# A streaming-encoder block on one core: the planned order's rule for the port that VectorE and GpSimd share, gating and pooling matrices in fp32, and two pieces of GpSimd's work given to VectorE

## The chip, the cores and the metric

The kernel runs on one NeuronCore of a Trainium2 chip. The core has a matrix engine (TensorE, "PE" in the profile, with its weight loads shown apart as "PEld"), VectorE ("DVE"), ScalarE ("ACT"), GpSimd ("POOL") and SyncE ("SP"), whose queue issues every DMA of this kernel. Each engine takes its instructions strictly in the order in which the program gives them; semaphores make an engine wait for others. The metric is the device time in microseconds of one execution; lower is better. The kernel before takes 1183.75 us (median of 3 runs, 1181.96 to 1185.1).

## The reference, cut to what matters

One layer of an encoder over 1024 positions of 1024 channels, all in fp32. Three sub-layers follow one another, each normalised before and after and added to the stream. The change touches the first one, and of the second the weights of its values.

```python
h = rms_norm(x, pre_mix_g)                 # 1024 x 1024
z = h @ w_in + b_in                        # columns: A 256, B 2*384, C 2*384
# A: pooling. p = trailing-window mean (2, 4, 8, 16) - token, then a 64x64 matrix per group
y_a = einsum(p, pool_w) * pool_scale
# B: gating. z_b = gelu(z_b); u, v = split(z_b)
v = layer_norm(v, sg_ln_g, sg_ln_b)        # (v - mean) * rstd * g + b over 384 columns
sv = einsum('hts,bnshd->bnthd', tril(sg_w), v) + sg_b   # 4 heads of 96, blocks of 128 positions
y_b = u * sv
# C: GLU, causal depthwise convolution of 31 taps, LayerNorm, swish
x = x + rms_norm(concat(y_a, y_b, y_c) @ w_out, post_mix_g)
# second: 4-head cross-attention into 256 memory tokens: q = h@wq, k = m@wk, v = m@wv
# third:  square(relu(h @ w_ff1)) @ w_ff2, 4096 wide
```

## The kernel before, in words

**Products of split parts.** Nearly every fp32 matrix product is made of three faster ones. An fp32 operand is split into a `hi` part, which is the operand cast to the type fp32r (ACT's `copy`), and a `lo` part, operand minus `hi` (`lo_of`, a subtraction on VectorE or GpSimd). `mm3` then adds hi*hi, hi*lo and lo*hi into one PSUM bank. In the profile's names a tile `wk3h` is the upper part of block 3 of wk, `wk3l` its lower part.

**The stages.** In the program's order: norm and transposition of x (`norm_in`); the convolution's input columns (`za`, `zg`) and its gate; then per half of the sequence (`hf`) and pair of 128-position blocks (`pr`) the products with the other columns of w_in (`zb`), from which the pooling's input `zt` and the gating's `zz` (768 columns: u and v) are taken; then `pooled(hf)`; then the memory tokens `mT`, the keys (`mem_product("wk")`, matmuls `wkp`), the convolution's taps (`conv_taps`, on VectorE with PSUM accumulators `cacca`, `caccb`, `caccc`) and its norm (`conv_norm`: transposes `cnat`, statistics `cst`, the power `cr..r` on GpSimd, scaling `cn`, transposes back `cback`, sigmoids `csg`). The results lie in `yq`. Then the output projection (`om`, seven products in place of eight block products), the values of the memory (`mem_product("wv")`, matmuls `wvp`), the queries (`pq`), attention, the projection `ox` and the two large products of the MLP (`fx`, `fy`, `fz`, `g`).

**The gating norm.** Per block, VectorE takes mean and variance of v, GpSimd raises variance plus epsilon to -0.5 (`vr..r`), VectorE makes (v - mean) * rstd in one `tensor_scalar`, GpSimd multiplies with `sgn[:, 0]` and adds `sgn[:, 1]` (instructions `zz<-zz,sgn`), ACT casts to `vh`, and GpSimd subtracts to `vl`. Four heads then take `mm3` each per pair (matmuls `sv`, 192 columns), with the transposed lower-triangular matrices split into `swt`. VectorE adds `sgb` and multiplies with u, PE transposes the result (`ybt`), ACT copies it to `yq`.

**The pooling.** GpSimd adds up windows (`zw`), VectorE makes mean minus token (`zp`), ACT casts to `ph`, GpSimd subtracts to the lower part of `ph`, and `mm3` multiplies with the split block-diagonal matrix `pw` (matmuls `pya`).

**The weight rows.** `row_unit` (line 497 of the listing and after) loads one 128 x 1024 block of w_in, wk or wv, casts it on ACT and makes its lower part on GpSimd in two pieces of 512 columns: `zr0` to `zr7`, `wk0` to `wk7`, `wv0` to `wv7`.

**The order.** No order is written by hand. The program records every operation (class `Schedule`; `record` is called for each, so the profile shows line 162 for all of them), and `_order` plans it: it keeps for each engine the time at which it is free, and for each operation the time at which its inputs are ready. At each step every engine offers one operation (`pick`), the one with the earliest start, then with the earliest due time; of these offers the earliest is placed. Due times are worked back from PE's order of the pass before; PE itself goes by the program's order. `_cost` gives each operation a duration. The planner knows that VectorE and GpSimd share a port to SBUF: operations with the flag `port` (GpSimd's `tensor_tensor`; VectorE's with two wide operands in SBUF, or its one-operand copies and scalings) can't run at the same time as one of the other engine, so an operation that needs the port is given a start no earlier than `port[e]`, the end of the other engine's last one. Six passes are made and the best is taken. Tiles lie in 50 slots of 4 KB per partition, which are given out in the planned order, as are 8 PSUM banks. A DMA may be issued at most 150 PE operations ahead of its place in the program (`LEAD`).

Of the kernel before, what the change touches and what calls it, by code (L numbers as in the profile page):

```python
# [16 lines left out]
P = 128  # L17
# [48 lines left out]
class Schedule:  # L66
# [136 lines left out]
    @staticmethod  # L203
    def _cost(eng, method, args, kw, ins):
        n = 1
        for d in args[0].shape[1:]:
            n *= d
        if method == "dma_start":
            return max(450.0, n * args[0].shape[0] * 4 / 220.0)
        size = lambda a: int(np.prod(a.shape[1:]))  # L210
        if eng == "pe":
            return max(109.0, 13.4 + n * 0.4167)
        wide = [a for a in ins if size(a) > 1]
        ptrs = len(ins) - len(wide) if n > 1 else 0
        if eng == "act":
            c = 51.0 + 0.833 * n + (0.0 if ins[0].space == bass.MemoryType.PSUM else 42.0)
            return c + 93.0 * min(ptrs, 1) + (93.0 if "accum_out" in kw else 0.0)
        if eng == "pool":
            if method == "tensor_tensor":
                return 520.0 if n < 17 else 60 + 2.4 * n  # L220
            return 60 + 1.0 * n
        n = max([n] + [size(a) for a in wide])
        psum = any(a.space == bass.MemoryType.PSUM for a in ins + [args[0]])
        if not psum and len(wide) == 1 and method in ("tensor_scalar", "tensor_scalar_mul",
                                                      "tensor_copy"):
            return 69 + 0.52 * n + 61.0 * ptrs
        return 69 + 1.042 * n + 61.0 * ptrs
# [20 lines left out]
    def _order(self, pe_order):  # L248
# [61 lines left out]
        def pick(e):  # L310
            b = None
            for i in ready[e]:
                op = ops[i]
                t0 = max(free[e], op.ready)
                if op.port and port[e] > t0:
                    t0 = port[e]
                ok = True
# [9 lines left out]
                if op.table and op.table != table:  # L327
                    t0 += 1283.0
                key = (t0, op.due, i)
                if b is None or key < b:  # L330
# [4 lines left out]
        while len(out) < n:  # L335
            b, be = None, None
            for e in self.ENG:
                if ready[e]:
                    k = pick(e)
                    if k is not None and (b is None or k < b):  # L340
                        b, be = k, e
            if b is None:
                raise RuntimeError("no instruction can be placed")
            t0, _, i = b
            op = ops[i]
# [54 lines left out]
def block_kernel(ctx: ExitStack, tc: tile.TileContext, x, mem, pre_mix_g, w_in, b_in, pool_w,  # L400
# [34 lines left out]
    def lo_of(eng, lo, src, hi):  # L435
        eng.tensor_tensor(lo, src, hi.bitcast(F32), ALU.subtract)

    def mm3(ps, a_hi, a_lo, b_hi, b_lo, first, last, more=False):

# [56 lines left out]

    def row_unit(name, w, r):
        def go():
# [4 lines left out]
            act.copy(hi, raw)  # L503
            for c in (slice(0, D // 2), slice(D // 2, D)):
                lo_of(pool, lo[:, c], raw[:, c], hi[:, c])
            return hi, lo
        return go

    units, made = {}, {}
    for j in range(3):  # L510
        units[f"zc{j}"] = col_unit(f"zc{j}", [(w_in, 1024 + j * P), (w_in, 1408 + j * P)], j == 0)
    for k in range(NK):
        units[f"zr{k}"] = row_unit(f"zr{k}", w_in, k)
    for k in range(NK):
        units[f"wk{k}"] = row_unit(f"wk{k}", wk, k)
    for k in range(NK):
        units[f"wv{k}"] = row_unit(f"wv{k}", wv, k)

# [178 lines left out]
    for h in range(NH):  # L697
        pe.transpose(ps[:, h * P:(h + 1) * P], sgr[:, h, :], ident)
    swt = slot("swt", [2, NH, P], F32R)
    act.copy(swt[:, 0], ps.rearrange("p (h t) -> p h t", h=NH))  # L700
    lo_of(dve, swt[:, 1], ps.rearrange("p (h t) -> p h t", h=NH), swt[:, 0])

    pwr = slot("pwr", [2, P])
    pool.memset(pwr, 0.0)
    for g in range(4):
        o = (g % 2) * 64
        sync.dma_start(pwr[o:o + 64, g // 2, o:o + 64], pool_w[0, g])
    pw = slot("pw", [2, 2, P], F32R)
    act.copy(pw[:, 0], pwr)
    lo_of(dve, pw[:, 1], pwr, pw[:, 0])  # L710
    inv = sc.tile(cp, [P, 2, 16], F32, "inv", 1, "inv")
# [8 lines left out]
    def pooled(hf):  # L720

        n = H + 16
        for m in range(2):
# [13 lines left out]
            for i in range(2):  # L737
# [4 lines left out]
                if hf == 0:  # L742
# [4 lines left out]
                                         ALU.mult, ALU.subtract)  # L747
            ph = slot(f"ph{m}{hf}", [2, H], F32R)
            act.copy(ph[:, 0, :], pt)
            lo_of(pool, ph[:, 1, :], pt, ph[:, 0, :])  # L750
            ps = bank(f"pya{m}{hf}")
            mm3(ps, pw[:, 0, m, :], pw[:, 1, m, :], ph[:, 0, :], ph[:, 1, :], True, True)
            act.activation(y_of(hf, m), ps, AF.Copy, scale=pscale[:, m:m + 1])

    for hf in range(2):
        for m in range(2):
            zaT[hf][m] = slot(f"zaT{hf}{m}", [H + 16])
        for pr in range(2):
            vh = slot(f"vh{hf}{pr}", [2, 384], F32R)
            vl = slot(f"vl{hf}{pr}", [2, 384], F32R)  # L760
            us = []
            zt = slot(f"zt{hf}{pr}", [2, 256])
            for i in range(2):
# [19 lines left out]
                r = rstd_of(f"vr{hf}{b}", mv[:, 1:2], 1)  # L783
                dve.tensor_scalar(v, v, mv[:, 0:1], r, ALU.subtract, ALU.mult)
                pool.tensor_tensor(v, v, sgn[:, 0, :], ALU.mult)
                pool.tensor_tensor(v, v, sgn[:, 1, :], ALU.add)
                act.copy(vh[:, i, :], v)
                lo_of(pool, vl[:, i, :], v, vh[:, i, :])
                us.append(zz)
# [8 lines left out]
            for h in range(NH):  # L798
                dst = pv[h // 2][:, (h % 2) * 192:(h % 2) * 192 + 192].rearrange(
                    "p (i c) -> p i c", i=2)  # L800
                c = slice(h * 96, (h + 1) * 96)
                mm3(dst, swt[:, 0, h, :], swt[:, 1, h, :], vh[:, :, c], vl[:, :, c], True, True)
            for i in range(2):
# [627 lines left out]
```

## Time and profile before

| what | value |
|---|---|
| median of 3 runs | 1183.75 us (1181.96 to 1185.1) |
| profiled execution | 1183.73 us, its span 1181.7 us |
| PE busy | 1148.9 us, 97%, 5339 matmuls |
| DVE busy | 914.2 us, 77% |
| ACT busy | 578.8 us, 49% |
| POOL busy | 260.0 us, 22%, 260 instructions |
| mean granted PE clock | 0.991 |
| HBM | 116.01 MB read, 46.14 MB written |

The profile is of one execution. Its span runs from the first to the last instruction. "Busy" is the time in which an engine had an instruction under way; the share is of the span. The granted clock is 1.00 at full speed, and it falls in a few stretches. The profile's rows name an instruction by its output and inputs (`out<-in`), with buffer numbers left out. GpSimd and VectorE are used all through the first 570 us; after that GpSimd has next to nothing to do until the last norm.

### The profile page before, as it was taken

The page shows a single profiled execution, that of the slowest core. Times are in us where ns is not written, and L with a number is a line of the kernel's source. Part 1 is how long each engine was busy: PE and PEld are TensorE (multiplying, and loading weights), DVE is VectorE, ACT ScalarE, POOL GpSimd, SP SyncE. Part 2 cuts the span into 40 slices and gives each one's busy share as a digit, 9 for nine tenths or more (in the row PEclk, how much of TensorE's full clock was granted, in tenths as well). Part 3 has the DMA queues.
Part 4 walks back from the last instruction along what each step waited for, and adds up shares of the span by engine and source line. Part 5 has one row for each costly group of instructions (what it writes and reads, how often), then busy time and mean ns, then how long its engine had stood idle before and what let it go on. Part 6 is the DMA issues. An engine that isn't in the chain of part 4 may idle for free.

```text
span 1181.7 us, 14682 instructions
## 1 busy us (share of the span) xinstructions
PE 1148.9 (97%) x5339; PEld 951.0 (80%) x5339; DVE 914.2 (77%) x1253; ACT 578.8 (49%) x1011; POOL 260.0 (22%) x260
## 2 busy tenths in 40 slices
PE   7999998899999999999999999999999999999997
PEld 6788787688877889788888888888888888888885
DVE  5499997599879877999999967657487945586936
ACT  5422245566974557838934433333346533345311
POOL 4451459501688302462100000000000000000001
PEclk9999999799999999999999999999999999999999
DMA  8310026104670413136224554533585445443533
GB/s 270 124 39 1 1 70 228 42 18 154 234 299 8 143 54 108 36 107 214 72 89 178 186 180 169 176 136 125 187 288 193 178 138 177 161 149 108 195 143 143
DMA packets 87078, 163.11 MB, mean 138 GB/s; under 512 B 6474, under 2 KB 29918, under 8 KB 87006
## 3 DMA queue, kind: packets, MB, share of 16 engines
q1 hardware_dynamic: 87006, 162.17, 39.3%
q8 instruction: 42, 0.69, 0.2%
q14 instruction: 30, 0.25, 0.1%
HBM read 116.01 MB, written 46.14 MB: 137 GB/s over the span
## 4 chain that ended last, share of the span: by engine, by line
PE 86%; DVE 8%; ACT 3%; issue 1%; POOL 1%; DMA 1%; DVEq 0%; POOLq 0%; ACTq 0%
PE g L162 26%; PE fx L162 14%; PE fz L162 7%; PE om L162 6%; PE pq L162 6%; PE ox L162 6%; PE zb L162 5%; PE fy L162 3%; PE zg L162 2%; PE za L162 2%; DVE cacca L162 2%; PE wkp L162 2%; PE o L162 2%; PE sc L162 2%; ACT junk L162 1%
## 5 line engine op out<-in xcount | busy, mean ns | idle before, releaser
L162 POOL TENSOR_TENSOR fr0r<-fr0e,half 128x1 f32<-128x1 f32 x1 | 0.9, 864 | 577.5 <-DVE fr0e L162 577.5
L162 DVE TENSOR_TENSOR acc<-acc,g 128x512 f32<-128x512 f32 x40 | 26.9, 685 | 54.3 <-PE g L162 54.3
L162 DVE TENSOR_TENSOR c<-c,fz 128x512 f32<-128x512 f32 x32 | 22.0, 686 | 44.2 <-PE fz L162 35.8
L162 ACT COPY c<-fx 128x512 f32<-128x512 f32 x48 | 28.0, 606 | 42.1 <-PE fx L162 39.7
L162 ACT ACTIVATE c<-fx 128x512 f32<-128x512 f32 x16 | 9.5, 596 | 54.3 <-PE fx L162 54.3
L162 ACT CAST w1o<-w1a 128x512 fp32r<-128x512 f32 x32 | 20.1, 637 | 29.3 <-issue 10.0
L162 DVE SCALAR_TENSOR_TENSOR c<-c 128x512 f32<-128x512 f32 x48 | 33.1, 691 | 0.4
L162 DVE SCALAR_TENSOR_TENSOR cacca<-hc,taps,cacca 128x511 f32<-128x511 f32 (+14 forms) x45 | 32.7, 755 | 0.0
L162 DVE SCALAR_TENSOR_TENSOR caccc<-hs,cws,caccc 128x511 f32<-128x511 f32 (+14 forms) x45 | 32.1, 747 | 0.0
L162 ACT ACTIVATE junk<-acc 128x512 f32<-128x512 f32 x16 | 10.1, 633 | 43.5 <-DVE acc L162 43.3
L162 DVE SCALAR_TENSOR_TENSOR caccb<-hc,taps,caccb 128x511 f32<-128x511 f32 (+13 forms) x42 | 30.8, 750 | 0.1
L162 PE MATMUL sc<-kv,q 128*128 128x256 f32 x192 | 28.4, 290 | 0.0
L162 PEld LDWEIGHTS sc<-kv,q 128*128 128x128 f32 x192 | 25.3, 191 | 0.6
L162 ACT CAST w1o<-w1c 128x512 fp32r<-128x512 f32 x32 | 19.7, 622 | 11.3 <-PE fx L162 4.8
L162 PE MATMUL fy<-h3a21h,w1o 128*128 128x512 f32 x64 | 25.1, 392 | 0.0
L162 PE MATMUL fz<-h3a30h,w1o 128*128 128x512 f32 x64 | 25.0, 391 | 0.0
L162 PE MATMUL fz<-h3a50h,w1o 128*128 128x512 f32 x64 | 24.9, 389 | 0.0
L162 PE MATMUL fy<-h3a20h,w1o 128*128 128x512 f32 x64 | 24.9, 389 | 0.0
L162 PE MATMUL fz<-h3a51h,w1o 128*128 128x512 f32 x64 | 24.9, 389 | 0.0
L162 PE MATMUL fz<-h3a31h,w1o 128*128 128x512 f32 x64 | 24.9, 389 | 0.0
L162 PE MATMUL fx<-h3a40h,w1o 128*128 128x512 f32 x64 | 24.9, 391 | 0.0
L162 PE MATMUL fx<-h3a70h,w1o 128*128 128x512 f32 x64 | 24.9, 391 | 0.0
(1668 smaller groups left out, 4192.9 us busy)
## 6 DMA issues: line engine op xcount, KB each, us to landing
ha<-scr_hid SPq DMA_DIRECT2D x56, 512.0 KB
scr_hid<-c SPq DMA_DIRECT2D x48, 256.0 KB
scr_hid<-sa SPq DMA_DIRECT2D x32, 256.0 KB
scr_hid<-sb SPq DMA_DIRECT2D x32, 256.0 KB
x<-in_x_dram SPq DMA_DIRECT2D x8, 512.0 KB
omwb<-in_w_out_dram SPq DMA_DIRECT2D x8, 512.0 KB
omx<-in_x_dram SPq DMA_DIRECT2D x8, 512.0 KB
scr_x<-omx SPq DMA_DIRECT2D x8, 512.0 KB
```

The source lines that it names most:

```text
L162: op.fn = lambda: f(*[put(a) for a in args], **{k: put(v) for k, v in kw.items()})
```

## The change

Five edits are made together.

1. In `pick`, the time at which an operation could start but for the port is kept (`came`). Between the engines' offers with the same start, the one that came first is placed first; only then do due times decide. Within one engine nothing changes.
2. `_cost` counts a matmul with fp32 moving operand as four passes.
3. Gating and pooling multiply in fp32 itself (`mm4`, one instruction of the program), without splitting: `swt` and `pwr` are used whole, `vv` takes the place of `vh` and `vl`, and the casts and subtractions of `vh`, `vl`, `ph`, `pw` and of `swt`'s lower part go.
4. The gating norm is made in two `scalar_tensor_tensor` on VectorE: (v - mean) * gain, then times rstd plus bias. The `tensor_scalar` and GpSimd's two `tensor_tensor` go. The power `vr..r` stays on GpSimd.
5. The lower parts of `wv0` to `wv7` are made on VectorE, in one piece of 1024 columns each. Those of `zr` and `wk` stay on GpSimd.

```diff
         if eng == "pe":
-            return max(109.0, 13.4 + n * 0.4167)
+            passes = 4 if method == "matmul" and args[1].dtype == F32 else 1
+            return passes * max(109.0, 13.4 + n * 0.4167)
...
                 t0 = max(free[e], op.ready)
-                if op.port and port[e] > t0:
-                    t0 = port[e]
                 ok = True
...
                     t0 += 1283.0
-                key = (t0, op.due, i)
+                came = t0
+                if op.port and port[e] > t0:
+                    t0 = port[e]
+                key = (t0, op.due, i, came)
...
-                    if k is not None and (b is None or k < b):
+
+                    if k is not None and (b is None or (k[0], k[3], k[1]) < (b[0], b[3], b[1])):
                         b, be = k, e
...
+    def mm4(ps, a, b, first=True, last=True):
+
+        pe.matmul(ps, a, b, start=first, stop=last)
...
-    def row_unit(name, w, r):
+    def row_unit(name, w, r, eng):
...
-            for c in (slice(0, D // 2), slice(D // 2, D)):
-                lo_of(pool, lo[:, c], raw[:, c], hi[:, c])
+            if eng is dve:
+                lo_of(dve, lo, raw, hi)
+            else:
+                for c in (slice(0, D // 2), slice(D // 2, D)):
+                    lo_of(pool, lo[:, c], raw[:, c], hi[:, c])
...
+    ZR, WK, WV = [pool] * NK, [pool] * NK, [dve] * NK
...
-    swt = slot("swt", [2, NH, P], F32R)
-    act.copy(swt[:, 0], ps.rearrange("p (h t) -> p h t", h=NH))
-    lo_of(dve, swt[:, 1], ps.rearrange("p (h t) -> p h t", h=NH), swt[:, 0])
+    swt = slot("swt", [NH, P])
+    act.copy(swt, ps.rearrange("p (h t) -> p h t", h=NH))
...
-    pw = slot("pw", [2, 2, P], F32R)
-    act.copy(pw[:, 0], pwr)
-    lo_of(dve, pw[:, 1], pwr, pw[:, 0])
...
-            ph = slot(f"ph{m}{hf}", [2, H], F32R)
-            act.copy(ph[:, 0, :], pt)
-            lo_of(pool, ph[:, 1, :], pt, ph[:, 0, :])
             ps = bank(f"pya{m}{hf}")
-            mm3(ps, pw[:, 0, m, :], pw[:, 1, m, :], ph[:, 0, :], ph[:, 1, :], True, True)
+            mm4(ps, pwr[:, m, :], pt)
...
-            vh = slot(f"vh{hf}{pr}", [2, 384], F32R)
-            vl = slot(f"vl{hf}{pr}", [2, 384], F32R)
+            vv = slot(f"vv{hf}{pr}", [2, 384])
...
-                dve.tensor_scalar(v, v, mv[:, 0:1], r, ALU.subtract, ALU.mult)
-                pool.tensor_tensor(v, v, sgn[:, 0, :], ALU.mult)
-                pool.tensor_tensor(v, v, sgn[:, 1, :], ALU.add)
-                act.copy(vh[:, i, :], v)
-                lo_of(pool, vl[:, i, :], v, vh[:, i, :])
+                dve.scalar_tensor_tensor(v, v, mv[:, 0:1], sgn[:, 0, :], ALU.subtract, ALU.mult)
+                dve.scalar_tensor_tensor(vv[:, i, :], v, r, sgn[:, 1, :], ALU.mult, ALU.add)
...
-                mm3(dst, swt[:, 0, h, :], swt[:, 1, h, :], vh[:, :, c], vl[:, :, c], True, True)
+                mm4(dst, swt[:, h, :], vv[:, :, c])
```

More of the change, by code (lines that the diff above doesn't have):

```diff
@@ L343, in _order @@
                 raise RuntimeError("no instruction can be placed")
-            t0, _, i = b
+            t0, _, i, _ = b
             op = ops[i]
@@ L512, in block_kernel @@
     for k in range(NK):
-        units[f"zr{k}"] = row_unit(f"zr{k}", w_in, k)
+        units[f"zr{k}"] = row_unit(f"zr{k}", w_in, k, ZR[k])
     for k in range(NK):
-        units[f"wk{k}"] = row_unit(f"wk{k}", wk, k)
+        units[f"wk{k}"] = row_unit(f"wk{k}", wk, k, WK[k])
     for k in range(NK):
-        units[f"wv{k}"] = row_unit(f"wv{k}", wv, k)
+        units[f"wv{k}"] = row_unit(f"wv{k}", wv, k, WV[k])
     def W(name):
```

## The prediction

> **What bounds the kernel now.** I read five views, in this order: the busy times, the stretches, the PE waits, the timelines of GpSimd and VectorE around the worst stretch, and the groups of instructions. The busy times first.
>
> ```profile
> PE 1148.9 (97%) x5339; PEld 951.0 (80%) x5339; DVE 914.2 (77%) x1253; ACT 578.8 (49%) x1011; POOL 260.0 (22%) x260
> ```
>
> PE is busy for 1148.9 of 1181.7 us. All idle time of PE together is 32.8 us, so no rearrangement of the other engines can bring more than that plus what a slowed clock costs. The question is where those microseconds lie. The next rows are stretches of the span: length, then the busy time of PE, PEld, DVE, ACT and POOL with their instruction counts, then the granted PE clock, DMA share and GB/s.
>
> ```profile
> ...
> 120.00:150.00 30.00, 28.87 (x137) 23.54 (x137) 29.51 (x58) 7.53 (x19) 13.19 (x16) 1.00 0.00 1
> 180.00:210.00 30.00, 25.82 (x124) 20.86 (x123) 19.24 (x40) 16.52 (x28) 27.10 (x24) 0.90 0.63 229
> 210.00:240.00 30.00, 24.83 (x120) 20.12 (x119) 18.61 (x40) 19.49 (x34) 12.03 (x14) 0.82 0.06 18
> 240.00:270.00 30.00, 30.00 (x134) 24.83 (x133) 28.89 (x33) 20.60 (x30) 0.00 (x0) 1.00 0.10 34
> 300.00:330.00 30.00, 29.27 (x141) 24.17 (x140) 24.60 (x32) 29.72 (x69) 19.24 (x16) 1.00 0.64 233
> 330.00:360.00 30.00, 29.38 (x138) 23.16 (x137) 21.89 (x19) 18.56 (x45) 26.01 (x17) 1.00 0.71 265
> 360.00:390.00 30.00, 27.27 (x117) 21.36 (x117) 26.30 (x18) 16.20 (x21) 18.62 (x10) 1.00 0.15 53
> 660.00:860.00 200.00, 200.00 (x882) 165.04 (x881) 135.65 (x197) 74.52 (x127) 0.00 (x0) 1.00 0.46 160
> ...
> ```
>
> From 660 to 860 us, 882 matmuls take 200.00 us, 0.227 us each, with no idle time: that is PE at its pace. Two neighbouring stretches are the exception: 180 to 240 us has 4.18 + 5.17 = 9.35 us of idle PE, and its clock was granted at 0.90 and 0.82, a deficit of (0.10 + 0.18) x 30 = 8.4 us. Together 17.75 us are lost there at most (idle time at low clock is counted twice, so a little less). 120 to 150 us loses 1.13 us, and 300 to 390 us loses 0.73 + 0.62 + 2.73 = 4.1 us at full clock. Three finer stretches place the first loss:
>
> ```profile
> ...
> 200.00:210.00 10.00, 6.05 (x23) 4.53 (x24) 5.26 (x16) 2.38 (x6) 8.67 (x8) 0.69 0.61 211
> 220.00:230.00 10.00, 5.78 (x41) 5.22 (x40) 6.68 (x13) 9.44 (x17) 2.04 (x2) 0.88 0.00 0
> 230.00:240.00 10.00, 9.05 (x38) 6.69 (x37) 9.12 (x25) 7.47 (x15) 2.33 (x4) 0.60 0.00 0
> ...
> ```
>
> 200 to 210 us loses 3.95 us idle and 0.31 x 10 = 3.1 us of clock, 7.05 us in all; 220 to 240 us loses 4.22 + 0.95 = 5.17 us idle and (0.12 + 0.40) x 10 = 5.2 us of clock, 10.4 us in all. In both the clock is low just after PE had idled. The waits of PE (us in total, times, longest) name the releasers:
>
> ```profile
> ...
> PE cnat L162 <- DVE kT L162: 4.2, 1, 4.2
> PE ybt L162 <- DVE zz L162: 2.7, 2, 2.0
> ...
> PE sv L162 <- POOL vl L162: 1.4, 1, 1.4
> ...
> ```
>
> `sv`, the gating matmul, waits for GpSimd's `vl`; `ybt`, the transpose of the gated values, waits for the VectorE gate behind that matmul; `cnat`, the first transpose of the convolution's norm, waits for a bank that VectorE's `kT` has to leave. What held those two engines is seen in the timelines of GpSimd and of VectorE (start, length, engine, instruction, in brackets the idle time before it and what ended it):
>
> ```profile
> ...
> 198.76 2.40 POOL L162 TENSOR_TENSOR vl<-zz,vh 128x384 fp32r<-128x384 f32 x2
> 201.12 1.76 POOL L162 TENSOR_TENSOR ph<-zp,ph 128x512 fp32r<-128x512 f32 x1
> 204.21 1.27 POOL L162 TENSOR_TENSOR ph<-zp,ph 128x512 fp32r<-128x512 f32 x1 [1.33 <-ACT ph L162]
> 205.44 1.27 POOL L162 TENSOR_TENSOR wk3l<-wk3r,wk3h 128x512 fp32r<-128x512 f32 x1
> ...
> 214.11 2.54 POOL L162 TENSOR_TENSOR wk7l<-wk7r,wk7h 128x512 fp32r<-128x512 f32 x2
> 216.60 0.55 POOL L162 TENSOR_TENSOR cr00r<-cr00e,half 128x1 f32<-128x1 f32 x1
> ...
> ```
>
> ```profile
> ...
> 217.19 0.68 DVE L162 TENSOR_SCALAR cn<-cnat,cmv,cr00r 128x384 f32<-128x384 f32 x1 [11.84 <-POOL cr00r L162]
> ...
> ```
>
> GpSimd takes everything in its planned order: the last gating splits, the pooling splits, then the lower parts of `wk3` to `wk7` in one row from 205.44 to 216.65 us, and only then the 0.55 us power `cr00r`. VectorE stands 11.84 us before `cn` for that power, with the splits of w_out, and later `kT`, queued behind it. So the loss from 200 to 240 us begins in GpSimd's backlog.
>
> **GpSimd: what it loses.** The groups (instructions | busy us, mean ns of one):
>
> ```profile
> ...
> L162 POOL TENSOR_TENSOR zz<-zz,sgn 128x384 f32<-128x384 f32 x16 | 17.2, 1076 | 6.2 <-DVE zz L162 4.9 <-DVE memr1e L162 0.7 <-PE wkp L162 0.3
> ...
> L162 POOL TENSOR_TENSOR vl<-zz,vh 128x384 fp32r<-128x384 f32 x8 | 8.6, 1081 | 4.1 <-ACT vh L162 4.1
> ...
> L162 POOL TENSOR_TENSOR ph<-zp,ph 128x512 fp32r<-128x512 f32 x4 | 6.1, 1524 | 4.8 <-ACT ph L162 4.8
> ...
> ```
>
> All 16 multiply-adds of the gating norm, 8 `vl` and 4 `ph` go: 17.2 + 8.6 + 6.1 = 31.9 us. Between 186 us and `cr00r` there are four of the first, two of the second and two of the third: 4 x 1.08 + 2 x 1.08 + 2 x 1.52 = 9.5 us, and the wait of 1.33 us for ACT's cast of `ph` goes with them. `wk3l` to `wk7l`, which stay on GpSimd, and `cr00r` behind them can come about 10 us sooner. For PE I take this in two places. From 200 to 210 us, `sv` no longer waits for `vl` and the later `wkp` matmuls are ready to fill the time of the gate: 6 of 7.05 us come back. From 220 to 240 us, VectorE is no longer held, but the norm's own chain (statistics, power, scaling, transposing back, sigmoid) stays, and the first output products cover it only where the order puts them between: I take half, 5 of 10.4 us. Sum -11, bounds 0 and -17.4. From 120 to 150 us the first gating pair has the same chain of three GpSimd steps and two casts: -0.8 of 1.13, bounds 0 and -1.1.
>
> **VectorE: what it gains.** A step of the new norm is one scalar_tensor_tensor over 384 columns. The kernel before has none of that width; the two nearest have 512 and 96 columns and stand in the groups below (first the page's, then those of 80 to 240 us). The tensor_scalar that goes is in the timeline:
>
> ```profile
> ...
> L162 DVE SCALAR_TENSOR_TENSOR c<-c 128x512 f32<-128x512 f32 x48 | 33.1, 691 | 0.4
> ...
> ```
>
> ```profile
> ...
> L162 DVE SCALAR_TENSOR_TENSOR zz<-sv,vec,zz 128x96 f32<-128x96 f32 x32 | 7.6, 324 | 0.8 <-PE sv L162 0.8
> ...
> L162 DVE TENSOR_TENSOR omww10l<-omwb,omww10h 128x1024 fp32r<-128x1024 f32 x1 | 1.2, 1215 | 0.0
> ...
> L162 DVE TENSOR_TENSOR swt<-ps_sgw,swt 128x512 fp32r<-128x512 f32 x1 | 0.7, 700 | 0.0
> ...
> ```
>
> ```profile
> ...
> 192.53 0.47 DVE L162 TENSOR_SCALAR zz<-zz,vmv,vr13r 128x384 f32<-128x384 f32 x1
> ...
> ```
>
> By the line through 324 ns at 96 and 691 ns at 512, 384 columns cost about 0.58 us (an estimate). Per block 2 x 0.58 - 0.47 = +0.69, for 8 blocks +5.5; `swt`'s lower part (0.70) goes, and that of `pw`, half as wide, is left at nothing: +4.8 us. Up to the end of the convolution VectorE is nearly full (29.51 of 30 in the stretch from 120 us). What covers it is that nobody is waiting for its last result:
>
> ```profile
> ...
> L162 PEld LDWEIGHTS cnat<-ident,cs x24: 139/163/231, 198.3 to 231.2; 128*128 128x128 f32 x24
> L162 PE MATMUL cnat<-ident,cs x24: 270/347/448, 198.6 to 231.4; 128*128 128x128 f32 x24
> ...
> L162 DVE SCALAR_TENSOR_TENSOR cs<-caccc,cb,cua x3: 736/739/750, 141.8 to 184.1; 128x512 f32<-128x512 f32 x3
> ...
> ```
>
> The last `cs` is complete at 184.1 + 0.74 = 184.8 us, and its reader `cnat` starts at 198.6: 13.8 us of cover. Cost taken 0; without the cover +4.8; below nothing it cannot be, VectorE does more. The lower parts of `wv` move as well: 8 instructions of 1024 columns at 1.215 us (the `omww10l` row), 9.7 us, into the hand-over from the output projection to the query product. VectorE idles 5.40 + 8.11 = 13.5 us between 300 and 360 us, and GpSimd, which loses 16 pieces there, has been busy 19.24 + 26.01 us. Behind these splits on VectorE stand the residuals, and for those waits the query product. I take -1 of the 4.1 us lost from 300 to 390; bounds -4.1 and +9.7.
>
> **PE: what it gains.** Gating goes from 48 matmuls to 16 in fp32, pooling from 12 to 4. Their pace before is in PE's timeline:
>
> ```profile
> ...
> 150.23 0.61 PE L162 MATMUL sv<-vh,swt 128*128 128x192 f32 x4
> 150.68 0.39 PE L162 MATMUL sv<-vl,swt 128*128 128x192 f32 x2
> ...
> ```
>
> Four `sv` matmuls start within 0.45 us: 0.112 us each; a pooling matmul of 512 columns has the 0.227 us from above. Before: 48 x 0.112 + 12 x 0.227 = 8.1 us. No fp32 product that is not a transpose is in this trace. With one pass each 2.7 us remain (-5.4); with four, as the changed planner line counts, 16 x 4 x 0.112 + 4 x 4 x 0.227 = 10.8 (+2.7); with each of four at double price 21.6 (+13.5). I take four, +2.7: three products of split parts stood for the same precision, so far fewer is unlikely, and PE has little idle time to hide it.
>
> A rule that speaks against the change: the Trainium skill, "TensorE: Matmul & The Clock Gate", section "Weight-path perf modes — Fast Weight Load (FWL) and DoubleRow", says that weights load fast only when their type is not FP32, and measures about a factor of two. The trace has loads of both types:
>
> ```profile
> ...
> L162 PEld LDWEIGHTS sv<-vh,swt x32: 187/192/192, 119.4 to 202.2; 128*128 128x128 f32 x32
> ...
> ```
>
> Against 192 ns (median) for the split weights stand 163 ns for `cnat`'s fp32 ones above: no penalty, though those are transposes and the rule is not refuted for products.
>
> **The order's new tie rule, and the rest.** First come, first served only decides between engines whose next starts are equal; it adds no instruction. Its bounds: the wait of 2.73 us from 360 to 390 us gone, or another as long. I take 0. The casts that ACT loses cost nothing either way (49% busy). No load is added or removed on SP's queue; one slot per pair instead of two, and none for `pw` and `ph`, lets loads start no later: 0.
>
> **Sum.** -11 - 0.8 - 1 + 2.7 = -10.1 us. The profiled run took 1183.73 us around its span of 1181.7, and the median is 1183.75, so the same sum holds: **1173.6 us**. PE is dense from 390 us to its end, so what is won earlier reaches the end.
>
> **Rivals.** (1) *Nearly all comes back*: both stretches fill and the hand-over loses nothing: -17.4 - 1.1 - 4.1 + 2.7 = -19.9, 1163.9 us. For it: the power comes 10 us sooner and half of the loss is only slow clock after idling. Against: the norm's chain stays.
> (2) *VectorE takes GpSimd's place*: the output product starts sooner, but VectorE, busy 28.89 of 30 from 240 us on, can't deliver its splits sooner, and the idle time moves there. Only the direct waits for `vl` and the gate go, 1.4 + 2.0, and 0.8: -4.2 + 2.7 = -1.5, 1182.3 us. For it: those 28.89 us. Against: 60 - 37.85 = 22.15 us of idle VectorE from 180 to 240 (19.24 + 18.61 busy).
> (3) *Slower*: the `wv` splits on VectorE delay the residuals. Price: 9.7 us, and on each of the eight one wait for a GpSimd piece of about 1.27 us (the last `ph`), 10.2 us. If nothing of it fits into the 13.5 us of idle VectorE, because these are gaps of a chain, it is +19.9 with no credit of 1 there: 1194.5 us. It decides once more than about 14 us of it show. Against: the idle time is larger than the work, and GpSimd's load there falls.
> (4) *Double loads*: 16 x 4 x 0.112 = 7.2 us more for the gating, which is paced by its weight loads and not by its columns (192 of 512 columns would take 0.085 of the 0.227 us, and take 0.112); 1180.8 us. It is the one that the rule above would give; the `cnat` row is against it.
>
> **How the numbers follow.** Chances: forecast 0.60, (1) 0.12, (2) 0.14, (3) 0.08, (4) 0.06. A difference under 0.3% (3.55 us) can't be told from none with this kernel; faster means under 1180.2. The forecast is faster in nearly all of its weight (0.58), (1) in all, (2) and (4) in a little (0.04); within 0.3% fall most of (2) and (4), 0.16; slower are (3) and 0.02 of (2) and (4), 0.10. Range: below to rival (1), 1163; above past (2) to 1186, where about +12.5 of the unknown costs have come in against the forecast.
>
> **What would show it.** In the changed profile: no GpSimd work between `zw` and `wk7l` but splits; `cr00r` near 206 us or sooner and the 11.84 us wait of `cn` mostly gone; `sv` released by VectorE; 180 to 240 us with under 8 us lost and fewer slow-clock stretches; `sv` at about 0.45 us per fp32 matmul; no new wait of `wvp` for VectorE above 1 us. The forecast is wrong if the output product doesn't start some 10 us sooner than 236 us, if idle PE appears between 240 and 390 us, or if an fp32 gating matmul takes over 0.9 us.

## The result and the profile after

The changed kernel takes **1170.87 us** (median; 1170.44 to 1171.63) against 1183.72 us for the kernel before on the same chip (1181.96 to 1185.1): a ratio of 0.9893, 95% interval 0.9876 to 0.991, or 12.85 us less. Predicted were 1173.6 us, with 1163 to 1186 as the range. The sum came out nearly right, but the terms did not: the hand-over and the fp32 products were mis-sized, the tie rule was put at nothing, and together they cancel. That the total is near is luck.

The busy times of the changed kernel:

```profile
PE 1144.6 (98%) x5319; PEld 944.7 (81%) x5319; DVE 912.8 (78%) x1267; ACT 571.5 (49%) x998; POOL 208.5 (18%) x216
```

GpSimd works 51.5 us less, and VectorE as long as before. PE is busy 4.3 us less: its 20 instructions fewer bring nothing of that (the fp32 ones take longer, below), but less of its work runs at a low clock (0.97 was granted from 180 to 240 us, 0.86 before). The stretches (length, busy PE, PEld, DVE, ACT and POOL, granted PE clock, DMA share, GB/s), first those that answer to the prediction's:

```profile
...
0.00:120.00 120.00, 110.31 (x553) 91.91 (x553) 91.75 (x164) 44.49 (x71) 43.76 (x80) 1.00 0.32 107
120.00:150.00 30.00, 30.00 (x140) 24.29 (x138) 29.90 (x59) 6.07 (x17) 9.49 (x14) 1.00 0.00 1
180.00:210.00 30.00, 29.80 (x143) 23.83 (x142) 28.55 (x40) 17.10 (x27) 29.59 (x22) 1.00 0.70 249
210.00:240.00 30.00, 25.45 (x127) 18.90 (x126) 26.05 (x56) 23.12 (x41) 8.45 (x10) 0.94 0.00 1
...
```

```profile
...
180.00:240.00 60.00, 55.25 (x268) 42.74 (x267) 54.60 (x95) 40.22 (x68) 38.04 (x31) 0.97 0.35 125
240.00:300.00 60.00, 59.75 (x272) 48.65 (x271) 56.67 (x69) 38.73 (x67) 7.20 (x8) 1.00 0.37 132
300.00:390.00 90.00, 90.00 (x419) 73.94 (x418) 77.78 (x77) 63.76 (x130) 45.86 (x31) 1.00 0.52 193
390.00:590.00 200.00, 198.50 (x1026) 167.79 (x1025) 167.85 (x242) 138.78 (x302) 52.46 (x38) 1.00 0.26 90
...
```

And two stretches of the kernel before that the prediction did not show:

```profile
...
0.00:120.00 120.00, 111.20 (x551) 92.75 (x552) 91.52 (x159) 45.42 (x73) 48.81 (x86) 1.00 0.32 107
...
390.00:590.00 200.00, 199.00 (x1030) 168.55 (x1028) 177.98 (x238) 140.35 (x304) 63.75 (x44) 1.00 0.29 101
...
```

I read a loss off each as the prediction did: idle PE plus missing clock times length. From 180 to 240 us 17.75 us were lost before; now it is 0.20 up to 210 us and 4.55 + 0.06 x 30 = 6.35 after it, 6.55 in all: -11.2. From 300 to 390 us the 4.1 us are gone. From 120 to 150 us the 1.13 us are gone as well, but a wait of 0.46 us for the first gated values has moved ahead of 120 us:

```profile
...
119.03 0.30 PE L162 MATMUL ybt<-ident,zz 128*128 128x128 f32 x1 [0.46 <-DVE zz L162]
...
```

That makes -0.7. Up to 120 us PE idles 9.69 us against 8.80; the other 0.4 lies in the first 20 us of the span, where the kernel with edit 5 alone (below) idles as long. New are 0.25 us from 240 to 300 and 0.5 from 390 to 590 us, and PE's own work has grown by 0.5 us (below). Sum: -11.2 - 4.1 - 0.7 + 0.4 + 0.25 + 0.5 + 0.5 = -14.35. Idle time at a low clock is counted twice in it, 9.35 x 0.14 = 1.3 us before and 4.55 x 0.06 = 0.3 now; -13.3 is left, and 12.85 was measured. In every experiment below such a reading comes out too favourable by some microseconds: it says where time is lost, and only roughly how much.

Where the work lies in the worst stretch now, by PE's and GpSimd's timelines (start, length, instruction, in brackets the idle time before it and its end's cause):

```profile
...
212.69 1.14 PE L162 MATMUL cnat<-ident,cs 128*128 128x128 f32 x9
...
217.23 0.61 PE L162 MATMUL kt<-ident,kn 128*128 128x128 f32 x4
218.57 0.66 PE L162 MATMUL kt<-ident,kn 128*128 128x128 f32 x4 [0.72 <-DVE cn L162]
...
222.36 1.98 PE L162 MATMUL pya<-zp,pwr 128*128 128x512 f32 x2 [0.88 <-DVE cn L162]
224.13 2.51 PE L162 MATMUL cback<-ident,cn 128*128 128x128 f32 x12
...
227.16 0.50 PE L162 MATMUL om<-omww10h,oma10h 128*128 128x512 f32 x1
...
```

```profile
...
207.18 2.27 POOL L162 TENSOR_TENSOR wk7l<-wk7r,wk7h 128x512 fp32r<-128x512 f32 x1
...
215.13 0.55 POOL L162 TENSOR_TENSOR cr00r<-cr00e,half 128x1 f32<-128x1 f32 x1 [3.68 <-DVE cr00e L162]
...
```

The output product starts at 227.16 instead of 236 us, 8.8 us sooner. The power `cr00r` no longer stands behind a backlog: GpSimd waits for it (3.68 us, released by VectorE). But it comes at 215.13, not near 206 us: the norm's first transposes `cnat`, which began at 198.6 us before, now begin at 212.69, behind most of the key products. Between the norm's steps stand transposes of the keys (`kt`) and, at 222.36, the last pooling product `pya`. The whole order is another, and that is what the prediction had not reckoned with.

### The profile page after: what moved, and what is told of

Its sections match the earlier page's. It is cut to its first block, busy times and chain, and to the rows that moved or that the text cites. A ratio compares the mean times of both kernels' runs of the same rounds, so it can differ in the third digit from the quotient of the medians.

```text
span 1169.5 us, 14585 instructions
## 1 busy us (share of the span) xinstructions
PE 1144.6 (98%) x5319; PEld 944.7 (81%) x5319; DVE 912.8 (78%) x1267; ACT 571.5 (49%) x998; POOL 208.5 (18%) x216
## 4 chain that ended last, share of the span: by engine, by line
PE 80%; DVE 5%; ACT 4%; issue 1%; POOL 0%; DVEq 0%; ACTq 0%; POOLq 0%
PE g L162 26%; PE fx L162 13%; PE fz L162 7%; PE pq L162 7%; PE zb L162 5%; PE ox L162 5%; PE om L162 4%; PE fy L162 3%; PE sc L162 2%; PE o L162 2%; PE wvp L162 2%; PE wkp L162 2%; ACT oxh L162 1%; ACT junk L162 1%; PE pT L162 1%
## 5 line engine op out<-in xcount | busy, mean ns | idle before, releaser
L162 DVE TENSOR_TENSOR w1o<-w1a,w1o 128x512 fp32r<-128x512 f32 x32 | 21.7, 686 | 5.8 <-ACT w1o L162 5.6
L162 PE MATMUL fx<-h3a10h,w1o 128*128 128x512 f32 x64 | 24.9, 389 | 0.0
L162 PE MATMUL fx<-h3a11h,w1o 128*128 128x512 f32 x64 | 24.9, 389 | 0.0
```

The source lines that it names most:

```text
L162: op.fn = lambda: f(*[put(a) for a in args], **{k: put(v) for k, v in kw.items()})
```

## The experiments

The five edits fall into three parts: **T**, the tie rule (edit 1); **G**, fp32 products with their planner cost and the norm on VectorE (edits 2, 3, 4); **W**, the lower parts of `wv` on VectorE (edit 5). The diffs are cut to the lines that matter.

### Each part alone, and all without the tie rule

```diff
 T alone, on the kernel before
+                came = t0
+                if op.port and port[e] > t0:
+                    t0 = port[e]
+                key = (t0, op.due, i, came)
...
+                    if k is not None and (b is None or (k[0], k[3], k[1]) < (b[0], b[3], b[1])):
 W alone, on the kernel before
+            if name.startswith("wv"):
+                lo_of(dve, lo, raw, hi)
 G + W: the changed kernel without the tie rule
-                    if k is not None and (b is None or (k[0], k[3], k[1]) < (b[0], b[3], b[1])):
+                    if k is not None and (b is None or k < b):
 G alone: that, and
-    ZR, WK, WV = [pool] * NK, [pool] * NK, [dve] * NK
+    ZR, WK, WV = [pool] * NK, [pool] * NK, [pool] * NK
```

Expected of T alone:

> The kernel before with the new tie rule alone (edit 1). Parts theory (each part of the gain comes from work taken off GpSimd, the tie rule adds nothing): 1183.7 us within 2, PE's lost time from 300 to 390 us still 4 us and from 180 to 240 us still about 17. Order theory (the gain is the better order at the shared port): 1177 us or less, with the loss from 300 to 390 us under 1.5 us.

Expected of W alone:

> The kernel before with the values' split on VectorE alone (edit 5). Parts theory: 1178 us, -6, all of it between 300 and 390 us, where idle PE falls from 4.1 us to under 1; 180 to 240 us still loses about 17 us. Order theory: 1183 us, because the splits alone only move a load from one engine at the port to the other.

Expected of G alone:

> The kernel before with fp32 gating and pooling and the norm on VectorE (edits 2, 3 and 4), old tie rule, values' split on GpSimd. Parts theory: 1177 us, -7, from 180 to 240 us; idle PE from 300 to 390 us still about 4 us. Order theory: 1181 us or more.

Expected of G + W:

> The changed kernel with the old tie rule (edits 2 to 5 without 1). Parts theory: 1171 us within 2. Order theory: 1177 us or more.

Measured against 1182.74 us of the kernel before, with the two pairs that followed (T + G and T + W, against 1183.43) and the changed kernel (against 1183.72). The losses are read off the stretches as above:

| parts | median us | ratio (95%) | lost 180-240 | 240-300 | 300-390 |
|---|---|---|---|---|---|
| none | 1182.74 | | 17.8 | 0 | 4.1 |
| T | 1194.96 | 1.0104 (1.0089 to 1.012) | 14.5 | 6.6 | 7.4 |
| W | 1182.07 | 0.9991 (0.9982 to 0.9999) | 16.0 | 0.6 | 2.0 |
| G | 1186.35 | 1.0027 (1.0018 to 1.0037) | 14.5 | 0 | 7.1 |
| G + W | 1179.81 | 0.9968 (0.9956 to 0.9981) | 14.5 | 0 | 1.4 |
| T + G | 1179.92 | 0.9973 (0.9962 to 0.9984) | 4.9 | 0.5 | 6.1 |
| T + W | 1183.74 | 1.0 (0.9991 to 1.0009) | 17.3 | 0.6 | 0 |
| T + G + W | 1170.87 | 0.9893 (0.9876 to 0.991) | 6.6 | 0.3 | 0 |

My theory, that G brings the 11 us from 180 to 240 us by itself, fell: G alone brings 3.3 there and is slower in all. No part alone makes the kernel faster by over 0.3%, and the tie rule alone makes it 12.2 us slower, while on top of the other two it brings 1179.81 - 1170.87 = 8.9 us. The single effects (+12.2, -0.7, +3.6) add up to +15; the three together give -12.85. By the medians W brings 0.7 us alone, 6.5 with G, 11.2 with T and 9.1 with both; so no part has a price of its own. The rival theory, that the better order at the port is the gain, expected 1177 us or less of T alone and fell with its 1194.96 us.

The three columns don't add up to the times. Against the kernel before, each row's columns give 2 to 7 us more gain, or less loss, than its medians do (T + G: -10.4 against -3.5). What makes up the rest is not shown.

T alone loses where it was not looked for. Its stretches, and PE's longest wait (total, times, longest):

```profile
...
240.00:300.00 60.00, 54.03 (x242) 44.47 (x241) 50.33 (x62) 37.69 (x62) 7.33 (x7) 0.99 0.34 116
300.00:390.00 90.00, 87.07 (x397) 71.69 (x396) 73.84 (x66) 61.23 (x132) 70.15 (x42) 0.95 0.44 162
...
```

```profile
...
PE om0t L162 <- DVE omt L162: 6.0, 1, 6.0
...
```

PE stands 6.0 us before the transposes `om0t`, with the last part of the output projection queued behind them. With W, or with G, the loss from 240 to 300 us is 0.6 us or less.

G + W has the same operations as the changed kernel. Its PE timeline, to be laid beside the one above, and a line of GpSimd's:

```profile
...
206.67 1.02 PE L162 MATMUL pya<-zp,pwr 128*128 128x512 f32 x2
...
215.29 0.27 PE L162 MATMUL cnat<-ident,cs 128*128 128x128 f32 x1
215.39 1.47 PE L162 MATMUL kt<-ident,kn 128*128 128x128 f32 x12
216.70 1.36 PE L162 MATMUL cnat<-ident,cs 128*128 128x128 f32 x11
220.38 0.52 PE L162 MATMUL cnat<-ident,cs 128*128 128x128 f32 x3 [2.31 <-DVE cr03e L162]
...
225.56 0.44 PE L162 MATMUL cback<-ident,cn 128*128 128x128 f32 x2 [2.27 <-DVE kT L162]
...
232.29 0.77 PE L162 MATMUL om<-omww10h,oma10h 128*128 128x512 f32 x1 [1.39 <-DVE cmv L162]
...
```

```profile
...
218.93 0.55 POOL L162 TENSOR_TENSOR cr00r<-cr00e,half 128x1 f32<-128x1 f32 x1 [7.09 <-DVE cmv L162]
...
```

The norm stands behind the key products here too, without the tie rule: its first transpose comes at 215.29 us (with G alone at 217.5). GpSimd has no backlog either: it waits 7.09 us (with G alone 10.04) before `cr00r`, and yet the power comes at 218.93 (with G alone 221.16), later than in the kernel before. What differs is the filling. In G + W the last pooling product runs at 206.67 us and 12 key transposes in a row at 215.39, before the norm's work proper, and inside the norm PE waits 2.31, 2.27 and 1.39 us for VectorE with nothing to fill them. In the changed kernel `kt` and `pya` are the fillers, the norm's first transpose starts 2.6 us sooner, and the output product 5.1 us sooner. This is read off two timelines; which tie the planner decides otherwise to get there was not followed.

### Two parts together

```diff
 T + G: the changed kernel, with
-    ZR, WK, WV = [pool] * NK, [pool] * NK, [dve] * NK
+    ZR, WK, WV = [pool] * NK, [pool] * NK, [pool] * NK
 T + W: the kernel before, with edits 1 and 5
```

> The changed kernel with the values' split back on GpSimd (edits 1 to 4 without 5). Fit theory (the tie rule pays only where GpSimd has little left to ask of the port): 1178 us or more, with the loss in the hand-over from the output projection to the queries back at 4 us or more. Sum theory (tie rule -9 once the gating is off GpSimd, whatever the values do): 1175 us within 2. Draw theory (each edit makes the planner draw another order, and the time falls where the draw falls): no particular value.

> The kernel before with edits 1 and 5: new tie rule, values' split on VectorE, gating and pooling as before. Fit theory: GpSimd still has the gating, so the loss between the first product for the keys and the first for the output stays above 13 us, and the time is 1180 us or more. Sum theory: 1173 us. Draw theory: no particular value.

```profile
...
180.00:240.00 60.00, 55.12 (x273) 42.88 (x272) 55.86 (x96) 41.10 (x69) 38.31 (x32) 1.00 0.36 127
240.00:300.00 60.00, 59.46 (x269) 48.45 (x269) 55.29 (x64) 39.70 (x73) 12.87 (x11) 1.00 0.38 131
300.00:390.00 90.00, 85.66 (x388) 68.79 (x387) 71.19 (x64) 58.47 (x118) 64.07 (x41) 0.98 0.50 184
...
```

```profile
...
180.00:240.00 60.00, 49.28 (x232) 37.95 (x232) 48.35 (x83) 37.46 (x61) 49.78 (x39) 0.89 0.36 131
...
300.00:390.00 90.00, 90.00 (x427) 74.53 (x426) 83.25 (x81) 67.79 (x142) 47.70 (x30) 1.00 0.53 193
...
```

The first fence is T + G, the second T + W. The gain of 180 to 240 us comes with T and G together, in full and without W (4.9 us lost); with T and W there is none (17.3), GpSimd being busy 49.78 us of the 60 there. The gain of 300 to 390 us needs W: 0 lost with it beside T, 6.1 without. The fit theory's bounds hold in both kernels; the sum theory (1175 and 1173 us) fell.

### Is it the rule, or only another order?

```diff
 the rule turned round, in the changed kernel
-                    if k is not None and (b is None or (k[0], k[3], k[1]) < (b[0], b[3], b[1])):
+                    if k is not None and (b is None or (k[0], -k[3], k[1]) < (b[0], -b[3], b[1])):
 fp32 products priced as measured, in the changed kernel
-            passes = 4 if method == "matmul" and args[1].dtype == F32 else 1
-            return passes * max(109.0, 13.4 + n * 0.4167)
+            if method == "matmul" and args[1].dtype == F32:
+                return 2 * max(109.0, 4.0 + n * 0.8333)
+            return max(109.0, 13.4 + n * 0.4167)
```

> The changed kernel with the tie rule turned round: of two offers with the same start, the one that came last is placed first. Fit theory: further from what the port does, so slower than with the old rule, 1181 us or more. Draw theory: anywhere from 1171 to 1190, and not ranked by how well the rule fits the port.

> The changed kernel with the planner's cost of an fp32 product set to what the trace of the changed kernel shows (two passes at half rate: 0.33 us for 192 columns in place of 0.44, 0.86 in place of 0.91 for 512). The instructions are the same, only the planned order can differ. Fit theory: within 2 us of 1171. Draw theory: more than 3 us off, either way.

Last come, first served takes 1206.91 us (ratio 1.0196, 1.0182 to 1.0209), 27.1 us more than deciding by due times. Its PE waits:

```profile
...
PE pq L162 <- DVE vm L162: 9.8, 1, 9.8
...
PE pq L162 <- DVE qc L162: 5.0, 1, 5.0
PE om L162 <- DVE kT L162: 4.7, 1, 4.7
...
```

With the truer price for fp32 the planner makes another order: 1176.92 us (0.9928, 0.9907 to 0.995). Its six runs fall into two groups: two take 1170.4 and 1171.2 us, as long as the changed kernel, and four 1176.5 to 1178.0. So the order is not worse in itself; something in four of its runs costs some 6 us. The profile is of the upper group (1177.98 us); it loses 16.9 us from 180 to 240 us. VectorE's timeline and GpSimd's there, and PE's wait:

```profile
...
190.95 7.58 DVE L162 SCALAR_TENSOR_TENSOR zz<-zz,vmv,sgn 128x384 f32<-128x384 f32 x1
...
```

```profile
...
191.04 1.05 POOL L162 TENSOR_TENSOR zw<-zw 128x525 f32<-128x525 f32 x1
192.06 1.28 POOL L162 TENSOR_TENSOR wk4l<-wk4r,wk4h 128x512 fp32r<-128x512 f32 x1
193.31 2.54 POOL L162 TENSOR_TENSOR wk5l<-wk5r,wk5h 128x512 fp32r<-128x512 f32 x2
195.82 1.28 POOL L162 TENSOR_TENSOR wk6l<-wk6r,wk6h 128x512 fp32r<-128x512 f32 x1
197.06 1.06 POOL L162 TENSOR_TENSOR zw<-zaT 128x527 f32<-128x527 f32 x1
...
```

```profile
...
PE sv L162 <- DVE vv L162: 4.7, 1, 4.7
...
```

One VectorE instruction of 0.6 us lasts 7.58 us while GpSimd runs six instructions at its full pace. It is a step of the gating norm, and PE waits 4.7 us for that norm's result `vv`; in the changed kernel the list of PE's waits has none for `vv`. The kernel with the turned-round rule has two more of this kind (6.41 and 5.22 us). None is in the traces of the other kernels, where the two engines take turns. Is the shared port not first come, first served? The next runs ask that.

As to the heading's question: turning the rule round costs more than leaving it out, as the fit theory expected (1181 us or more). But that theory also expected the truer price within 2 us of 1171, and four of the six runs there are not; and the rule alone, which fits the port as well, costs 12.2 us. That the rule pays because it fits the port is not shown; that this order pays is.

### The port by itself

```diff
 first: GpSimd's eight subtractions of a burst write one tile
+    g.tensor_tensor(gc, ga, gb, ALU.subtract)
 then: eight tiles
+    g.tensor_tensor(gs[i], ga, gb, ALU.subtract)
 VectorE meanwhile, after a spacer of growing length
+    v.scalar_tensor_tensor(o[:, :384], va[:, :384], one[:, 0:1], vb[:, :384], ALU.subtract, ALU.mult)
```

> This program computes nothing of the block: its output is a copy of x, so only its trace says anything. GpSimd runs 80 bursts of eight subtractions of 128x512 from SBUF, in half of them with a multiplication of 128x1 after every second one; VectorE, released with the burst, first copies from PSUM for a time that grows from burst to burst, then gives one instruction with SBUF operands (scalar_tensor_tensor of 384 columns, tensor_tensor of 1024 or 384, tensor_scalar of 384, or three scalar_tensor_tensor of 256 in a row). Theory 'first come, first served' (the planner's): every VectorE instruction with two SBUF inputs waits for at most the one GpSimd instruction under way, so none lasts more than its own time plus 1.27 us: scalar_tensor_tensor of 384 up to 1.9 us, tensor_tensor of 1024 up to 2.5 us. Theory 'GpSimd can keep the port' (from the 7.58 us instruction of the run with the two-pass cost): in a good part of the bursts the instruction lasts through several of the eight, 3 to 9 us. If it happens only with the 128x1 instructions in the stream, as two of the three seen so far have them at their start, only that half of the bursts shows it.

> This program computes nothing of the block either: its output is a copy of x. As the port measurement before it, with one change of conditions: there GpSimd's eight subtractions all wrote one tile, and each started 0.078 us after the one before had ended; here they write eight tiles, so that each should start some 0.03 us before the one before has ended, as in the stretch with the 7.58 us instruction (191.045 to 198.117 us there). VectorE's instruction comes at 28 moments, 0.05 us apart, over the length of one subtraction; it is a scalar_tensor_tensor of 384 columns, a tensor_tensor of 1024, or two scalar_tensor_tensor in a row; half of the bursts have 128x1 multiplications in them. Theory 'the gap lets VectorE in': without it some or most of the VectorE instructions last through several of the eight, 3 to 10 us; in the 0.078 us gap none lasted over 2.3 us. Theory 'a race at the hand-over': only instructions that come within about 0.1 us of a GpSimd start are kept waiting, about 2 of 28 moments. Theory 'first come, first served after all, and the 7.58 us came from something else in that kernel': none lasts over 2.5 us.

The second one's groups (duration in ns, shortest, median, longest):

```profile
...
L82 DVE SCALAR_TENSOR_TENSOR o_stt<-va,one,vb x56: 607/1090/1737, 5.3 to 1816.0; 128x384 f32<-128x384 f32 x56
...
L77 DVE TENSOR_TENSOR o_tt<-va,vb x56: 1215/1633/2324, 15.6 to 1826.8; 128x1024 f32<-128x1024 f32 x56
...
L80 DVE SCALAR_TENSOR_TENSOR o_chain<-va,one,vb x56: 474/956/1607, 26.8 to 1838.3; 128x256 f32<-128x256 f32 x56
...
L66 POOL TENSOR_TENSOR gs<-ga,gb x1344: 1253/1258/2327, 4.3 to 1844.9; 128x512 f32<-128x512 f32 x192
...
```

The longest wait is 1737 - 607 = 1.13 us, less than one GpSimd instruction (1.258 us), whether GpSimd's instructions leave a gap or not; in the first measurement the longest scalar_tensor_tensor of 384 columns lasted 1.60 us. So in both measurements the port goes first come, first served, instruction by instruction, as the planner has it. The theory that GpSimd keeps it through a gapless row fell. What made one instruction last 7.58 us stays open; so does whether it makes the upper group of those runs, since no trace of the lower group exists. Only the size fits: PE's wait of 4.7 us against some 6 us between the groups.

### The norm's place, and one more candidate

```diff
 the norm's multiply and add on GpSimd, in the changed kernel
-                dve.scalar_tensor_tensor(v, v, mv[:, 0:1], sgn[:, 0, :], ALU.subtract, ALU.mult)
-                dve.scalar_tensor_tensor(vv[:, i, :], v, r, sgn[:, 1, :], ALU.mult, ALU.add)
+                dve.tensor_scalar(v, v, mv[:, 0:1], r, ALU.subtract, ALU.mult)
+                pool.tensor_tensor(v, v, sgn[:, 0, :], ALU.mult)
+                pool.tensor_tensor(vv[:, i, :], v, sgn[:, 1, :], ALU.add)
 three wk rows on VectorE, with fp32 products priced as measured
-    ZR, WK, WV = [pool] * NK, [pool] * NK, [dve] * NK
+    ZR, WK, WV = [pool] * NK, [pool, pool, pool, dve, pool, dve, pool, dve], [dve] * NK
```

> The changed kernel with the multiply and the add of the gating norm back on GpSimd (VectorE: subtract and scale in one tensor_scalar, as before), but the products in fp32 and no split of vv, ph, swt and pw. If it is the norm's way off GpSimd that makes the tie rule pay, GpSimd keeps 16 instructions of 1.08 us, four of them between 186 us and cr00r; 13 to 16 us are lost between the first key product and the first output product, and the time is 1177 to 1182. If the removed splits and casts alone make the room, 7 to 9 us are lost there and it is 1170 to 1174.

> The changed kernel with the planner's fp32 product priced at two passes, as the trace shows it (0.325 us for 192 columns), and the lower parts of three of the eight wk rows (3, 5, 7) on VectorE instead of GpSimd, so that GpSimd has no row of eight port instructions in the key products. If VectorE's 7.58 us instruction is what puts the run with the two-pass cost into its slower group, all runs here are in one group at 1166 to 1171, and no VectorE instruction in 180 to 215 us lasts over 2.6 us. If the order itself is what costs there, or VectorE (28 of 30 us busy from 180 us on) becomes the bound, 1174 to 1180.

With the norm on GpSimd: 1178.89 us (0.9964, 0.995 to 0.9978), 8.0 us more than the changed kernel. 7.69 + 0.06 x 60 = 11.3 us are lost from 180 to 240 us:

```profile
...
180.00:240.00 60.00, 52.31 (x254) 41.67 (x253) 45.56 (x86) 38.02 (x65) 43.16 (x36) 0.94 0.33 115
...
```

So, taken away last, the norm's place makes 4.7 of the 11.2 us there, and the removed splits with the tie rule the other 6.4; I had expected more of the norm (13 to 16 lost). Of the 8.0 us, 1.4 lie between 120 and 150 us, where the changed kernel loses nothing, and 1.8 between 390 and 590 us (3.27 us idle against 1.5). The candidate takes 1176.26 us (0.9937, 0.9922 to 0.9952). Its runs are one group, 1174.5 to 1177.2, and its VectorE has no instruction kept waiting long in the profile, yet it is as slow as the upper group with the 7.58 us one. It has another wait:

```profile
...
226.16 0.69 DVE L162 TENSOR_TENSOR kT<-kt,kT 128x512 fp32r<-128x512 f32 x1 [4.79 <-ACT kT L162]
...
```

The norm starts early there, its power comes at 201.5 us, VectorE is through with its splits at 221.4 us and stands 4.79 us for the keys. Of all the orders this is the closest to the one that the prediction had in mind, with the power some 15 us sooner than before; PE still loses 8.77 + 0.06 x 60 = 12.4 us from 180 to 240 us. Neither of the two beats the changed kernel.

## Why the prediction was right, and where it was not

**What bounds the kernel** held: PE has no idle time worth naming behind 390 us, so what was won before reached the end. Of the signs against the forecast, one came in part: the output product starts 8.8 us sooner, and not some 10.

**"Sum -11" for GpSimd's backlog**: measured -11.2 by the stretches, and 8.8 by the start of the output product, by an incomplete cause. The first place, 200 to 210 us, gave nearly all of its 7.05 us (6 were taken), the second 10.4 - 6.35 = 4.0 of the 5 taken. But the step "`wk3l` to `wk7l`, which stay on GpSimd, and `cr00r` behind them can come about 10 us sooner" kept the old order in mind and failed: `wk7l` is complete 7.2 us sooner (209.45 against 216.65), but `cr00r` came only 1.5 us sooner than at 216.60. What holds it is PE's new order, with the norm's transposes behind the key products, and no longer GpSimd. That new order comes with G already (`cr00r` at 221.16 us, after 10.04 us of waiting), and with it alone 3.3 us come back. The rest needs the tie rule beside it, in whose order other work of PE fills the norm.

**"I take 0" for the tie rule**, bounds of 2.7 us each way, is the step that failed worst: +12.2 us alone, -8.9 on top of the others. The sentence "it adds no instruction" is true and beside the point: a rule of the planner can move every instruction behind the first tie it decides.

**"-1 of the 4.1 us" at the hand-over** is a mis-sized term: all 4.1 came, the end of the bounds, and on top of T and G the move of the `wv` splits brings 9.1 us of the time. The doubt was rival (3), that the `wv` splits on VectorE would delay the residuals; W alone, at 0.9991, shows no such price.

**"-0.8" from 120 to 150 us**: 0.7; a wait of 0.46 us is left, ahead of the stretch.

**"I take four, +2.7"** for the fp32 products is a mis-sized term. The rows:

```profile
...
L162 PEld LDWEIGHTS sv<-vv,swt x32: 186/190/190, 116.1 to 198.2; 128*128 128x128 f32 x32
L162 PE MATMUL sv<-vv,swt x32: 323/326/408, 116.1 to 198.3; 128*128 128x192 f32 x32
...
```

```profile
...
197.19 1.46 PE L162 MATMUL sv<-vv,swt 128*128 128x192 f32 x8
...
```

```profile
...
L162 PE MATMUL pya<-zp,pwr x8: 592/631/1127, 150.5 to 223.3; 128*128 128x512 f32 x8
...
150.46 1.02 PE L162 MATMUL pya<-zp,pwr 128*128 128x512 f32 x2
...
```

Each fp32 product of the program is two instructions (32 for the 16 gating products, 8 for the 4 of the pooling). Eight of 192 columns take 1.46 us, the last of them 0.326, so (1.46 - 0.326) / 7 = 0.162 us each, 0.32 us per product where 0.45 was forecast; two of 512 columns start 1.02 - 0.592 = 0.43 us apart. In all 32 x 0.162 + 8 x 0.43 = 8.6 us against 8.1: +0.5. The Trainium skill, "Perfetto Trace Analysis", section "Engine Utilization", gives half the array's output rate for FP32_LOW_HIGH; no run here shows whether these products are in that mode, but each of their two instructions keeps half the pace, with 0.43 us for 512 columns against 0.227 of the split parts, and the product as a whole a quarter. The forecast's four passes are right for 512 columns (0.86 against 0.91 us) and too many for 192 (0.32 against 0.45). The loads took 190 ns (median) against 192 before, so rival (4) did not happen; as both types load alike, the rule behind it shows no effect here.

**VectorE's "+4.8, cost taken 0"** held in the changed kernel: the list of PE's waits has none for `vv`. A step takes 0.607 us where nothing is in its way (the port measurement's row; 0.58 was estimated), and three of the 16 take 1.22 to 1.66 us, near 190 us, beside a busy GpSimd. With G alone the cost was not 0: PE waits 1.7 us for `vv`. With the norm back on GpSimd the kernel is 8.0 us slower. Rival (2) did not happen although VectorE is busy 54.60 of the 60 us from 180 to 240 us, 16.75 more than before.

**The sum** was right by cancellation: the tie rule's share was booked under GpSimd's relief, the hand-over brought 3.1 us more than taken, and the fp32 products cost 2.2 less; against that stand 0.75 us of new losses, 0.4 in the first 20 us and the 1.0 us counted twice.

## What to carry to other kernels

Where a planner orders the work, an edit to its rules or costs has no price of its own: the same rule cost 12.2 us in one setting and brought 8.9 in another, and a truer cost gave an order that took 6 us more in four of six runs. Such an edit is forecast with a wide range on both sides, and tried with and without each of its companions, since a part that loses alone can be the one that makes the rest pay. A relieved engine need not bring time: with G alone GpSimd stood idle 10 us before the power that it had delayed, and most of the time came back only in an order that had work to fill the next wait. Look for what can fill that, and not only for the engine that was late.

## What the runs showed of the hardware

- Two engines on the port. In both measurements a VectorE instruction with two operands in SBUF waits for at most the GpSimd instruction under way (1.13 us at most, of 1.258), and the reverse (GpSimd's 1.258 us became up to 2.327). The Trainium skill, "SBUF — State Buffer", section "Who interferes with whom", says that a VectorE instruction with two inputs in SBUF contends with a GpSimd one that reads SBUF, and that the order of issue decides which is blocked; both measurements agree. Not covered by it, and not explained by them, are the three VectorE instructions of 7.58, 6.41 and 5.22 us in two of the kernels.
- An fp32 product on PE is two instructions. At 512 columns each takes 0.43 us, about twice the 0.227 of the split parts' type, and the product 0.86 us against 3 x 0.227 = 0.68 of three split ones. At 192 columns it takes 0.32 us, about what three split ones take (3 x 0.112). The casts and subtractions around them go.
